# Scaling of x by ScalarE alone in the opening of a gated FFN trunk layer, with the turns of ktiles 8 to 11 moved to the second block's sums

## The chip, the core and the metric

The kernel runs on one core of a Trainium2 chip. The metric is the device time of one execution in microseconds (us); the kernel before has a median of 1994.59 us over three runs.

## What is computed

One decoder layer on x of 256 tokens by 2048 channels in float32: a SwiGLU feed-forward block, a mixer, and a second feed-forward block. Before each, x is normalised and modulated by a vector c. Only the start concerns the change:

```python
mod = (silu(c) @ w_ada + b_ada).reshape(B, 9, 1, D)       # w_ada: 2048 x 18432
h = rms_norm(x, g_ffn1) * (1 + mod[:, 1]) + mod[:, 0]
g, u = split(h @ w_ffn1_gu, 2)                            # w_ffn1_gu: 2048 x 11264
x = x + 0.5 * mod[:, 2] * ((silu(g) * u) @ w_ffn1_down)   # w_ffn1_down: 5632 x 2048
```

No product of h can start before the columns of mod[:, 0] and mod[:, 1] that belong to its channels are summed over all 2048 rows of w_ada.

## The kernel before

**Tiling.** The 2048 channels are 16 ktiles of 128 rows; the 256 tokens are two tiles. Each float32 weight tile `raw` (128 x 1024 per ktile) is split into two reduced-precision halves: `wh`, cast by ScalarE (ACT, L285), and `wl = raw - wh`, by VectorE (DVE, L289). h is split likewise into `hh` and `hl`. TensorE (PE) adds three products per weight tile and token tile, wh·hh, wh·hl and wl·hh, two banks each, all on L304: 12 products of 512 columns for one ktile.

**Order of the products in the opening.** Because the modulation columns arrive in blocks, the first FFN's products run in segments `segs` of (column tile, ktile from, ktile to). The first six segments take ktiles 0 and 1 for six column tiles, the seventh takes ktiles 0 to 5 of column tile 6, and so on. When a segment is done its four PSUM banks are copied out by `evac` (L782), which sets its two groups of four banks free by turns.

**The modulation.** DVE multiplies each row tile of w_ada by its element of silu(c) (`cs`) and adds it up (`ada_acc`, L660/L662). PE then sums `acc` over its 128 rows by products with a column of ones: L764 for the first block (ktiles 0 and 1, all in the opening), L820 in `end` for later blocks. `ada_col` (L668 to L672) adds bias and gain into `mcol`. The second block is ktiles 2 to 5. Its 16 steps are spread over the first 12 turns.

**x.** `x_row` scales two ktiles of x by 1/rms, on ACT (L682) or with `True` as its last argument on DVE (L680). `x_T` turns them on PE by transposes (L688) into a bank, and `x_keep` (L741) copies the turned tile to `xT`, where `h_pair` (L694 to L697) later applies the modulation.

**Order by turns.** All engines follow the written order. `push` queues a ktile's products behind LAG = 2 others; each time one is taken, `turn_` also runs what `at(n, f)` planned for turn n. Turn 12 is where `end` of the second block stands, between the products of ktile 0 and of ktile 1 of the seventh segment.

**Loads.** Weight tiles of 1 MB, of w_ada and of w_ffn1_gu by turns, go through one pool of RAW = 6 buffers, issued in written order by SyncE (SP, L654 and L261); a load waits until the buffer's last reader is done.

Of the kernel before, what the change touches and what calls it, by code (L numbers as in the profile page):

```python
# [16 lines left out]
P = 128  # L17
D = 2048
S = 256
# [24 lines left out]
def trunk_layer(ctx, tc, x, c, w_ada, b_ada, g_ffn1, w_ffn1_gu, w_ffn1_down, g_mix, w_in,  # L44
                pool_mix, pool_scale, w_pool_up, q_gain, k_gain, sinks, rel_bias, w_attn_up,
                w_o, g_ffn2, w_ffn2_gu, w_ffn2_down, pool_w, onehot, out):
    nc = tc.nc
# [7 lines left out]
    def nm(s):  # L55
        uid[0] += 1
        return f"{s}_{uid[0]}"

    def t_(shape, tag, bufs=1, dt=F32):
        return sb.tile(list(shape), dt, tag=tag, bufs=bufs, name=nm(tag))  # L60
# [5 lines left out]
    def bank_at(i, shape):  # L66
        return ps.tile(list(shape), F32, tag=f"bank{i}", name=nm("bank"))

    def bank(shape=(P, CW)):
        for _ in range(4):  # L70
            rr[0] = (rr[0] + 1) % 4
            i = (1 - cur[0]) * 4 + rr[0]
            if i not in held:
                return bank_at(i, shape)
        raise RuntimeError("no bank free in the written order")
# [11 lines left out]
    KG, KB = 3 * KD + PW // P, 6 * KD  # L87
    gcol = const.tile([P, KG], F32, name="gcol")
    bcol = const.tile([P, KB], F32, name="bcol")
# [16 lines left out]
    def push(f):  # L106
        late.append([f])
        pushed[0] += 1
        while len(late) > LAG:
            turn_()  # L110
# [5 lines left out]
    def at(n, f, first=False):  # L116

        fs = plan.setdefault(max(n, done[0]), [])
        fs.insert(0, f) if first else fs.append(f)
# [410 lines left out]
    def turn_T(src, f0, n, actT, at_blocks, at_moves):  # L530


        z = []

        def blocks(t):
            if not z:
                z.append(t_([P, T, n], "raw", RAW))
            nc.vector.transpose(z[0][:, t, :], (src() if callable(src) else src)[:, t, 0:n])  # L538

        def move(i, j):  # L540
            k, m = f0 // P, n // P
            nc.scalar.copy(actT[32 * j:32 * j + 32, k:k + m, :].rearrange("p k (t i r) -> p k t i r", t=T, i=4)[:, :, :, i, :],  # L542
                           z[0][32 * i:32 * i + 32].rearrange("p t (k j r) -> p k t j r", j=4, r=32)[:, :, :, j, :])

        for t in range(T):
            at(at_blocks(t), lambda t=t: blocks(t))
        for q in range(16):
            at(at_moves(q), lambda q=q: move(q // 4, q % 4))
# [108 lines left out]
    def ada_acc(acc, r, kk, first):  # L657
        sc = cs[:, kk:kk + 1]
        if first:
            nc.vector.tensor_scalar_mul(acc, r, sc)  # L660
        else:
            nc.vector.scalar_tensor_tensor(out=acc, in0=r, scalar=sc, in1=acc, op0=ALU.mult, op1=ALU.add)  # L662

    def ada_col(k, n, j, sums):

        m = mcol[:, j, k:k + n]
        if j == 0:
            nc.vector.tensor_tensor(m, sums, bcol[:, k:k + n], ALU.add)  # L668
        else:
            nc.vector.scalar_tensor_tensor(out=m, in0=sums, scalar=1.0, in1=bcol[:, KD + k:KD + k + n],  # L670
                                           op0=ALU.add, op1=ALU.add)
            nc.vector.tensor_tensor(m, m, gcol[:, k:k + n], ALU.mult)  # L672

    def x_row(k, m=2, dve=False):

        xn = t_([P, T, m * P], "t2", T2)
        for t in range(T):
            a, sc = x_sb[:, t, k * P:(k + m) * P], st[:, 4, t:t + 1]
            if dve:
                nc.vector.tensor_scalar_mul(xn[:, t, :], a, sc)  # L680
            else:
                nc.scalar.activation(xn[:, t, :], a, AF.Copy, scale=sc)  # L682
        return xn

    def x_T(xn, b):
        for f in range(xn.shape[2] // P):
            for t in range(T):
                nc.tensor.transpose(b[:, f, t * P:(t + 1) * P], xn[:, t, f * P:(f + 1) * P], ident)  # L688
        return b
# [27 lines left out]
    def first_pe(kk, j):  # L717
        for a in range(2):
            nc.tensor.matmul(bsum[j][a], braw[kk // 4][:, kk % 4, j, a * P:(a + 1) * P], cs[:, kk:kk + 1],
                             start=kk == 0, stop=False)  # L720

    def first_dve(k0):
        for kk in range(k0 + 1, k0 + 4):
            ada_acc(acc0, braw[k0 // 4][:, kk - k0], kk, kk == 1)
# [10 lines left out]
    nc.vector.tensor_reduce(v2, ssq, AX.X, ALU.add)  # L735
    rsqrt2(v2, s0, r0, a0)
    nc.vector.tensor_tensor(st[:, 4, :], r0, a0, ALU.mult)
    xr = [x_row(0), x_row(2), x_row(4, 2, True)]

    def x_keep(b, k):  # L740
        nc.scalar.copy(xT[k], b)  # L741
# [4 lines left out]
    b0 = [x_T(xr[0][:, :, f * P:(f + 1) * P], bank_at(5 + 2 * f, (P, 1, S)))[:, 0, :] for f in range(2)]  # L746
    x_keep(x_T(xr[1], bank_at(6, (P, 2, S))), 2)
    x_keep(x_T(xr[2], bank_at(4, (P, 2, S))), 4)
    xr = [x_row(6, 2, True)]
    for j in (1, 0):  # L750
        first_pe(8, j)
    first_dve(8)
    xr += [x_row(8), x_row(10, 2, True)]
    xT[6] = t_([P, 2, S], "sl", 2)
    x_keep(x_T(xr[0], bank_at(6, (P, 2, S))), 6)
    b = bank_at(4, (P, KG + KB))
    nc.tensor.transpose(b[:, :KG], grow, ident[:KG, :KG])
    nc.tensor.transpose(b[:, KG:], brow, ident[:KB, :KB])
    for j in (1, 0):
        for kk in (13, 14, 15):  # L760
            ada_acc(acc0[:, j], braw[3][:, kk - 12, j], kk, False)
        first_pe(12, j)
        for a in range(2):
            nc.tensor.matmul(bsum[j][a], acc0[:, j, a * P:(a + 1) * P], ones_f[:, 0:1], start=False, stop=True)  # L764
        if j:
            b8 = x_T(xr[1], bank_at(6, (P, 2, S)))
    nc.vector.tensor_copy(gcol, b[:, :KG])
    nc.vector.tensor_copy(bcol, b[:, KG:])
    for j in (1, 0):
        for a in range(2):  # L770
            ada_col(a, 1, j, bsum[j][a])
    b10 = x_T(xr[2], bank_at(4, (P, 2, S)))
    xT[8], xT[10] = t_([P, 2, S], "sh", 2), t_([P, 2, S], "sl", 2)

    segs = [(i, 0, 2) for i in range(6)] + [(6, 0, 6)] + [(i, 2, 6) for i in (5, 4, 3, 2, 1)] + [(0, 2, 10)]
# [2 lines left out]
    def evac(i, k0, k1, s, t, c_):  # L778
        e = slice(c_ * CW, (c_ + 1) * CW)
        a, b = part[i][:, t, e], s.free(t, c_)  # L780
        if k0 == 0:
            nc.scalar.copy(a, b)  # L782
        else:
            nc.vector.tensor_tensor(a, b, a, ALU.add)  # L784
        if k1 == KD:
            if i % 2 or i == NS - 1:
                at(done[0] + 1, lambda a=a: nc.scalar.activation(a, a, AF.Silu))
            else:
                g = part[i + 1][:, t, e]
                nc.vector.tensor_tensor(g, a, g, ALU.mult)  # L790
# [14 lines left out]
    for k, n, need in ((2, 4, 14), (6, 4, 42), (10, 4, 70), (14, 2, 74)):  # L805
# [30 lines left out]
        while q < k + n:  # L836
# [9 lines left out]
                at(n_, lambda q=q, xn=xn, m=m: h_pair(x_T(xn[0], bank((P, m, S))), q, m))  # L846
            q += m

    cur[0] = 1
    n0 = 0  # L850
    for i, k0, k1 in segs:
        s = Set(w_ffn1_gu[0], KD, cols[i], hstat, late=True)
        if n0 == 0:
            raw = t_([P, 2, SW], "raw", RAW)
            for k in range(2):
                nc.sync.dma_start(raw[:, k, :], w_ffn1_gu[0][k * P:(k + 1) * P, cols[i][0]:cols[i][0] + SW])
            h = t_([P, 2, S], "t2", T2)
            wh = [s.hi_half(raw[:, 0, :])]
            mod = lambda a, f: nc.scalar.activation(a[:, f, :], b0[f], AF.Identity, scale=mcol[:, 1, f:f + 1],
                                                    bias=mcol[:, 0, f:f + 1])  # L860
            for f in range(2):
                mod(hh, f)
            wh.append(s.hi_half(raw[:, 1, :]))
            items = [s.prep(f, raw[:, f, :], given=wh[f]) for f in range(2)]
            for f in range(2):
                mod(h, f)
                nc.vector.tensor_tensor(hl[:, f, :], h[:, f, :], hh[:, f, :].bitcast(F32), ALU.subtract)
            x_keep(b8, 8)
            x_keep(b10, 10)

            def first_mm(f, *o, s=s, items=items):
                for t in range(T):
                    s.mm(items[f], t, None, 0, 2, o)

            push(lambda: first_mm(0, 0, 2))
            push(lambda: (first_mm(1, 0), first_mm(0, 1), first_mm(1, 1, 2)))
        else:
            s.pushes(k0, k1, k0, k1)
        n0 = pushed[0] - 1
        for q, (t, c_) in enumerate((t, c_) for t in range(T) for c_ in range(2)):  # L880
            at(n0 + (q // 2 if k1 > 2 else 0), lambda i=i, k0=k0, k1=k1, s=s, t=t, c_=c_: evac(i, k0, k1, s, t, c_), True)
        if k1 == KD and i in (4, 2, 0):
            turn_T(part[i + 1], i // 2 * SW, SW, actT, lambda t: n0 + 2 + t, lambda q: n0 + 5 + q // 2 * (2 if i else 1))
# [187 lines left out]
    for a in range(0, 8, 2):  # L1071
        with_bank(G[0] + 1 + a // 4, (P, 2, S), pool_prod(a),
                  lambda b, a=a: nc.vector.tensor_copy(pT_[0][:, a:a + 2, :], b))
        will(G[0] + 2 + a // 4, 0.7)
    for a in range(8):
        with_bank(G[0] + 4 + a // 2, (P, S), mix_prod(a),
                  lambda b, a=a: nc.scalar.activation(mixT[:, a, :], b, AF.Copy, scale=psc[:, a:a + 1]))
# [258 lines left out]
```

## Time and profile before

| | us |
|---|---|
| median of 3 runs (1993.12 to 1994.67) | 1994.59 |
| profiled execution, its own time | 1996.08 |
| span of that execution, first to last instruction | 1994.3 |
| PE busy | 1972.3 |
| DVE busy | 1513.6 |
| ACT busy | 1091.8 |

The trace gives starts from the span's first instruction. The profiled execution took 1.49 us more than the median run. A busy PE is only a PE with an instruction under way: the clock column PEclk tells whether it ran at its full level (1.00, 2.4 GHz) or at half (0.50, 1.2 GHz).

### The profile page before, as it was taken

The numbers are of one execution on the slowest core, as the hardware profiler recorded it, in microseconds if no ns is written. First come the engines' busy times: TensorE is split into PE (matmuls) and PEld (weight loads), VectorE is DVE, ScalarE is ACT, GpSimd is POOL, SyncE is SP. The second block draws the span as 40 slices with busy tenths as digits, with TensorE's granted clock in tenths as the row PEclk, the third lists the DMA queues.
The fourth block names the chain that finished last, engine by engine and source line by source line (L and its number), as shares of the span: only waits on it lengthen the run. The fifth ranks groups of instructions, "written<-read, shape, count | busy, mean of one in ns | idle before, by whom it ended". The sixth has DMA issues, their size and how long they took to land.

```text
span 1994.3 us, 23770 instructions
## 1 busy us (share of the span) xinstructions
PE 1972.3 (99%) x8873; PEld 1629.3 (82%) x8873; DVE 1513.6 (76%) x1749; ACT 1091.8 (55%) x1484; POOL 26.4 (1%) x51
## 2 busy tenths in 40 slices
PE   7999999999999999999999999999999999999999
PEld 6788888888788888888788888888888888888887
DVE  6898867989999978886889998888455454565655
ACT  6543457664664546446656455645564645565443
POOL 0000000000000000000000000000000000000000
PEclk9999999999999999999999999999999999999999
DMA  9989745899899966876688996598555645466652
GB/s 364 371 314 342 261 164 187 329 337 356 313 363 336 335 230 235 310 281 219 235 292 302 351 311 219 212 356 317 214 189 202 219 170 190 159 225 216 218 185 74
DMA packets 158212, 523.68 MB, mean 263 GB/s; under 512 B 9325, under 2 KB 21509, under 8 KB 157840
## 3 DMA queue, kind: packets, MB, share of 16 engines
q1 hardware_dynamic: 156464, 518.83, 72.7%
q0 software_dynamic: 1632, 3.34, 0.6%
q8 instruction: 69, 1.13, 0.2%
q14 instruction: 47, 0.39, 0.1%
HBM read 520.00 MB, written 2.12 MB: 262 GB/s over the span
## 4 chain that ended last, share of the span: by engine, by line
PE 96%; DVE 2%; DMA 1%; SPq 0%; issue 0%; ACT 0%; DVEq 0%; ACTq 0%
PE bank L304 93%; DVE acc L662 1%; DMA raw<-in_w_ffn_gu_dram 1%; DMA raw<-in_w_ada_dram 0%; DVE wl L289 0%; PE bank L1065 0%; SPq L654 0%; PE bank L820 0%; PE bank L196 0%; PE bank L195 0%; PE bank L357 0%; PE bank L1128 0%; PE bank L1092 0%; PE bank L999 0%; PE bank L1051 0%
## 5 line engine op out<-in xcount | busy, mean ns | idle before, releaser
L285 ACT CAST wh<-raw 128x1024 fp32r<-128x1024 f32 (+2 forms) x711 | 711.1, 1002 | 793.9 <-PE bank L304 739.7
L289 DVE TENSOR_TENSOR wl<-raw,wh 128x1024 fp32r<-128x1024 f32 (+2 forms) x713 | 823.5, 1157 | 418.4 <-ACT wh L285 413.7
L304 PE MATMUL bank<-wh,hl 128*128 128x512 f32 (+1 forms) x2088 | 653.6, 388 | 0.0
L304 PE MATMUL bank<-wh,hh 128*128 128x512 f32 (+1 forms) x2064 | 651.3, 390 | 0.3 <-DVE big L1099 0.3
L304 PE MATMUL bank<-wl,hh 128*128 128x512 f32 (+1 forms) x2064 | 647.5, 389 | 0.6 <-DVE wl L289 0.6
L304 PEld LDWEIGHTS bank<-wh,hl 128*128 128x128 f32 x2088 | 392.7, 188 | 81.3
L304 PEld LDWEIGHTS bank<-wl,hh 128*128 128x128 f32 x2064 | 388.2, 188 | 82.9 <-DVE wl L289 2.9
L304 PEld LDWEIGHTS bank<-wh,hh 128*128 128x128 f32 x2064 | 386.4, 189 | 80.2 <-issue 0.8
L230 DVE SCALAR_TENSOR_TENSOR acc<-raw,cs,acc 128x1024 f32<-128x1024 f32 (+1 forms) x231 | 279.8, 1211 | 0.8
L304 PE MATMUL bank<-wh,sh 128*128 128x512 f32 x656 | 203.7, 390 | 0.0
L304 PE MATMUL bank<-wh,sl 128*128 128x512 f32 x656 | 203.3, 389 | 0.0
L304 PE MATMUL bank<-wl,sh 128*128 128x512 f32 x656 | 203.1, 389 | 0.0
L304 PEld LDWEIGHTS bank<-wh,sl 128*128 128x128 f32 x656 | 123.0, 188 | 26.0 <-DVE sl L394 0.3
L304 PEld LDWEIGHTS bank<-wl,sh 128*128 128x128 f32 x656 | 123.1, 188 | 25.8
L304 PEld LDWEIGHTS bank<-wh,sh 128*128 128x128 f32 x656 | 122.6, 188 | 25.8 <-issue 0.4
L542 ACT COPY big<-raw 32x512 f32<-32x512 f32 (+1 forms) x208 | 121.9, 586 | 4.2
L662 DVE SCALAR_TENSOR_TENSOR acc<-raw,cs,acc 128x1024 f32<-128x1024 f32 (+2 forms) x74 | 77.7, 1052 | 1.0
L394 DVE TENSOR_TENSOR sl<-big,sh 128x512 fp32r<-128x512 f32 x82 | 56.2, 686 | 0.0
L393 ACT CAST sh<-big 128x512 fp32r<-128x512 f32 x82 | 50.7, 618 | 0.0
L784 DVE TENSOR_TENSOR big<-bank,big 128x512 f32<-128x512 f32 x56 | 36.4, 684 | 0.0
L329 ACT ACTIVATE junk<-x_sb 128x512 bf16<-128x512 f32 x24 | 15.2, 632 | 13.9 <-DVE x_sb L421 11.7
L538 DVE STREAM_TRANSPOSE raw<-sg 128x1024 f32<-128x1024 f32 (+1 forms) x20 | 22.7, 1133 | 0.0
(220 smaller groups left out, 802.7 us busy)
## 6 DMA issues: line engine op xcount, KB each, us to landing
raw<-in_w_ffn_gu_dram SPq DMA_DIRECT2D x175, 1024.0 KB, 5.3
raw<-in_w_ada_dram SPq DMA_DIRECT2D x112, 1024.0 KB, 7.2
raw<-in_w_ffn_down_dram SPq DMA_DIRECT2D x86, 1024.0 KB, 6.1
raw<-in_w_in_dram SPq DMA_DIRECT2D x48, 1024.0 KB, 6.8
raw<-in_w_ada_dram SPq DMA_DIRECT2D x64, 512.0 KB, 7.6
raw<-in_w_o_dram SPq DMA_DIRECT2D x15, 1024.0 KB, 7.8
raw<-in_w_pool_up_dram SPq DMA_DIRECT2D x8, 1024.0 KB, 7.9
raw<-in_w_attn_up_dram SPq DMA_DIRECT2D x8, 1024.0 KB, 6.9
```

The lines of the kernel that those rows point to most:

```text
L230: nc.vector.scalar_tensor_tensor(out=a[0], in0=r[0][:, kk % nk, :], scalar=sc, in1=a[0], op0=ALU.mult, op1=ALU.add)
L285: nc.scalar.copy(wh, raw_k)
L289: nc.vector.tensor_tensor(wl[:, e], raw_k[:, e], wh[:, e].bitcast(F32), ALU.subtract)
L304: nc.tensor.matmul(self.banks[t][i], a[:, sl], w[:, o], start=first and q == 0, stop=last and q == 2)
L329: nc.scalar.activation(junk, x_sb[:, t, n * CW:(n + 1) * CW], AF.Square, scale=(D / 2) ** -0.5, accum_out=ssq[:, t, n:n + 1])
L393: nc.scalar.copy(hi, src[:, k:k + n, :])
L394: nc.vector.tensor_tensor(lo, src[:, k:k + n, :], hi.bitcast(F32), ALU.subtract)
L538: nc.vector.transpose(z[0][:, t, :], (src() if callable(src) else src)[:, t, 0:n])
L542: nc.scalar.copy(actT[32 * j:32 * j + 32, k:k + m, :].rearrange("p k (t i r) -> p k t i r", t=T, i=4)[:, :, :, i, :], z[0][32 * i:32 * i + ...
L662: nc.vector.scalar_tensor_tensor(out=acc, in0=r, scalar=sc, in1=acc, op0=ALU.mult, op1=ALU.add)
L784: nc.vector.tensor_tensor(a, b, a, ALU.add)
```

## The change

All of `x_row` goes to ACT; three calls had been on DVE. The copies of the norm weights and biases (`gcol`, `bcol`) go from DVE to ACT. Scaling, turning and keeping ktiles 8 to 11 leave the opening: the rows are scaled at turn 10, turned at turn 12 just ahead of the second block's sums, and kept at turn 13 just ahead of what else stands there. The last products of the first block (`first_pe(12, j)`) now stand together ahead of the sums. The program holds the same calculations before and after.

```diff
@@ -735,7 +735,7 @@
     nc.vector.tensor_reduce(v2, ssq, AX.X, ALU.add)
     rsqrt2(v2, s0, r0, a0)
     nc.vector.tensor_tensor(st[:, 4, :], r0, a0, ALU.mult)
-    xr = [x_row(0), x_row(2), x_row(4, 2, True)]
+    xr = [x_row(0), x_row(2), x_row(4)]
 
     def x_keep(b, k):
         nc.scalar.copy(xT[k], b)
@@ -746,30 +746,27 @@
     b0 = [x_T(xr[0][:, :, f * P:(f + 1) * P], bank_at(5 + 2 * f, (P, 1, S)))[:, 0, :] for f in range(2)]
     x_keep(x_T(xr[1], bank_at(6, (P, 2, S))), 2)
     x_keep(x_T(xr[2], bank_at(4, (P, 2, S))), 4)
-    xr = [x_row(6, 2, True)]
+    xr = [x_row(6)]
     for j in (1, 0):
         first_pe(8, j)
     first_dve(8)
-    xr += [x_row(8), x_row(10, 2, True)]
     xT[6] = t_([P, 2, S], "sl", 2)
     x_keep(x_T(xr[0], bank_at(6, (P, 2, S))), 6)
     b = bank_at(4, (P, KG + KB))
     nc.tensor.transpose(b[:, :KG], grow, ident[:KG, :KG])
     nc.tensor.transpose(b[:, KG:], brow, ident[:KB, :KB])
+    nc.scalar.copy(gcol, b[:, :KG])
+    nc.scalar.copy(bcol, b[:, KG:])
+    for j in (1, 0):
+        first_pe(12, j)
     for j in (1, 0):
         for kk in (13, 14, 15):
             ada_acc(acc0[:, j], braw[3][:, kk - 12, j], kk, False)
-        first_pe(12, j)
         for a in range(2):
             nc.tensor.matmul(bsum[j][a], acc0[:, j, a * P:(a + 1) * P], ones_f[:, 0:1], start=False, stop=True)
-        if j:
-            b8 = x_T(xr[1], bank_at(6, (P, 2, S)))
-    nc.vector.tensor_copy(gcol, b[:, :KG])
-    nc.vector.tensor_copy(bcol, b[:, KG:])
     for j in (1, 0):
         for a in range(2):
             ada_col(a, 1, j, bsum[j][a])
-    b10 = x_T(xr[2], bank_at(4, (P, 2, S)))
     xT[8], xT[10] = t_([P, 2, S], "sh", 2), t_([P, 2, S], "sl", 2)
 
     segs = [(i, 0, 2) for i in range(6)] + [(6, 0, 6)] + [(i, 2, 6) for i in (5, 4, 3, 2, 1)] + [(0, 2, 10)]
@@ -845,6 +842,21 @@
                     n_ += 1
                 at(n_, lambda q=q, xn=xn, m=m: h_pair(x_T(xn[0], bank((P, m, S))), q, m))
             q += m
+
+
+    def two_rows():
+        xr[:] = [x_row(8), x_row(10)]
+
+    def two_turns():
+        xr[:] = [x_T(a, bank((P, 2, S))) for a in xr]
+
+    def two_keeps():
+        for a, k in zip(xr, (8, 10)):
+            x_keep(a, k)
+
+    at(10, two_rows)
+    at(12, two_turns, True)
+    at(13, two_keeps, True)
 
     cur[0] = 1
     n0 = 0
@@ -865,8 +877,6 @@
             for f in range(2):
                 mod(h, f)
                 nc.vector.tensor_tensor(hl[:, f, :], h[:, f, :], hh[:, f, :].bitcast(F32), ALU.subtract)
-            x_keep(b8, 8)
-            x_keep(b10, 10)
 
             def first_mm(f, *o, s=s, items=items):
                 for t in range(T):
```

On DVE in the opening these rows stood or now stand between the scaling by 1/rms and the first modulation column (acc_126 is the first block's sum, raw_110 to raw_116 its tiles of w_ada):

```order
-L680 TENSOR_SCALAR t_29_164<-x_sb,st 128x256 x2
 L662 SCALAR_TENSOR_TENSOR acc_126<-raw_110,cs,acc_126 128x512 x3
-L680 TENSOR_SCALAR t_34_192<-x_sb,st 128x256 x2
 L662 SCALAR_TENSOR_TENSOR acc_126<-raw_113,cs,acc_126 128x512 x3
-L680 TENSOR_SCALAR t_36_205<-x_sb,st 128x256 x2
 L662 SCALAR_TENSOR_TENSOR acc_126<-raw_116,cs,acc_126 128x256 x6
-L767 COPY gcol<-bank_215 128x56
-L768 COPY bcol<-bank_215 128x96
 L670 SCALAR_TENSOR_TENSOR mcol<-bank_124,bcol 128x1
 L672 TENSOR_TENSOR mcol<-mcol,gcol 128x1
```

Eight instructions leave DVE between those sums.

On ACT at turns 10 to 12 of the kernel before (raw_518 holds ktiles 0 and 1 of the seventh segment, banks 524 to 527 the sixth segment's result):

```order
L285 CAST wh_520<-raw_518 128x1024
L285 CAST wh_544<-raw_518 128x1024
L782 COPY gate_103<-bank_527 128x512
L782 COPY gate_103<-bank_526 128x512
L782 COPY gate_103<-bank_525 128x512
L782 COPY gate_103<-bank_524 128x512
L285 CAST wh_567<-raw_565 128x1024
```

and in the changed kernel, where raw_500 and banks 506 to 509 are the same things:

```order
L285 CAST wh_502<-raw_500 128x1024
L682 ACTIVATE t_107_526<-x_sb,st 128x256 x2
L682 ACTIVATE t_108_529<-x_sb,st 128x256 x2
L285 CAST wh_532<-raw_500 128x1024
L779 COPY gate_103<-bank_509 128x512
L779 COPY gate_103<-bank_508 128x512
L779 COPY gate_103<-bank_507 128x512
L779 COPY gate_103<-bank_506 128x512
L285 CAST wh_555<-raw_553 128x1024
```

Four scalings now stand between the two casts, ahead of the copies out of the banks.

On PE at turn 12, before (bank_587 takes the second block's sums; the trace lists each of these float32 products as two):

```order
L304 MATMUL bank_573<-wl_521,hh_105 128x512
L304 MATMUL bank_574<-wl_521,hh_105 128x512
L820 MATMUL bank_587<-ones_f,acc_290 128x1 x8
L304 MATMUL bank_571<-wh_544,hh_105 128x512
L304 MATMUL bank_572<-wh_544,hh_105 128x512
```

and after:

```order
L304 MATMUL bank_561<-wl_503,hh_105 128x512
L304 MATMUL bank_562<-wl_503,hh_105 128x512
L688 MATMUL bank_575<-ident,t_107_526 128x128 x4
L688 MATMUL bank_580<-ident,t_108_529 128x128 x4
L817 MATMUL bank_585<-ones_f,acc_272 128x1 x8
L304 MATMUL bank_559<-wh_532,hh_105 128x512
L304 MATMUL bank_560<-wh_532,hh_105 128x512
```

Eight transposes now stand between ktile 0's last product and the sums. Their banks come from the group that the sixth segment used: by the order of the pool, bank_575 follows bank_507, bank_580 follows bank_508, and bank_585 follows bank_509.

## Rows read from the trace of the kernel before

**Rows 1.** The page: the chain of work that ended last, as shares of the span by engine.

```profile
PE 96%; DVE 2%; DMA 1%; SPq 0%; issue 0%; ACT 0%; DVEq 0%; ACTq 0%
```

**Rows 2.** The chain that ended last in the opening, in order of time: start, us, what.

```profile
43.38 10.49 DMA raw<-in_w_ffn_gu_dram
...
65.92 2.41 PE bank L820 x16
68.33 59.97 PE bank L304 x252
```

**Rows 3.** Busy time by stretch: PE, PEld, DVE, ACT, POOL (instructions), PEclk, DMA share, GB/s.

```profile
30.00:36.00 6.00, 6.00 (x28) 4.98 (x27) 5.03 (x7) 4.31 (x8) 0.00 (x0) 1.00 1.05 397
...
48.00:54.00 6.00, 6.00 (x29) 4.95 (x27) 5.82 (x6) 3.17 (x7) 0.00 (x0) 1.00 1.04 396
...
66.00:72.00 6.00, 6.00 (x25) 5.23 (x26) 2.44 (x6) 3.13 (x6) 3.15 (x8) 0.60 1.04 395
...
76.00:80.00 4.00, 4.00 (x19) 3.33 (x18) 2.47 (x3) 2.11 (x2) 0.00 (x0) 1.00 0.84 284
```

**Rows 4.** SP's issues in order of time (start, us from the first issue's start to the last one's end), then the loads issued at 52.4 and at 53.07 us with us from issue to landing.

```profile
51.94 0.88 SPq L654 DMA_DIRECT2D raw<-in_w_ada_dram  x2
53.07 4.79 SPq L261 DMA_DIRECT2D raw<-in_w_ffn_gu_dram  x2
...
raw<-in_w_ada_dram SPq DMA_DIRECT2D x1, 512.0 KB, 9.5
...
raw<-in_w_ffn_gu_dram SPq DMA_DIRECT2D x1, 1024.0 KB, 11.3
```

**Rows 5.** ACT in order of time around the second block's sums: start, us, instructions, and in brackets the idle time before with what ended it.

```profile
53.96 2.00 ACT L285 CAST wh<-raw 128x1024 fp32r<-128x1024 f32 x2 [1.33 <-DMA raw<-in_w_ffn_gu_dram]
...
59.23 2.01 ACT L285 CAST wh<-raw 128x1024 fp32r<-128x1024 f32 x2 [1.16 <-DMA raw<-in_w_ffn_gu_dram]
61.45 2.06 ACT L782 COPY gate<-bank 128x512 f32<-128x512 f32 x4 [0.21 <-PE bank L304]
64.49 1.04 ACT L285 CAST wh<-raw 128x1024 fp32r<-128x1024 f32 x1 [0.98 <-DMA raw<-in_w_ffn_gu_dram]
68.83 1.09 ACT L694 ACTIVATE t<-big,mcol 128x256 f32<-128x256 f32 x2 [3.30 <-DVE mcol L668]
```

**Rows 6.** DVE in order of time in the same stretch.

```profile
55.04 1.23 DVE L289 TENSOR_TENSOR wl<-raw,wh 128x1024 fp32r<-128x1024 f32 x1 [0.80 <-ACT wh L285]
...
61.03 1.22 DVE L289 TENSOR_TENSOR wl<-raw,wh 128x1024 fp32r<-128x1024 f32 x1
62.17 1.28 DVE L662 SCALAR_TENSOR_TENSOR acc<-raw,cs,acc 128x1024 f32<-128x1024 f32 x1
63.36 1.22 DVE L289 TENSOR_TENSOR wl<-raw,wh 128x1024 fp32r<-128x1024 f32 x1
64.50 1.28 DVE L662 SCALAR_TENSOR_TENSOR acc<-raw,cs,acc 128x1024 f32<-128x1024 f32 x1
65.69 1.22 DVE L289 TENSOR_TENSOR wl<-raw,wh 128x1024 fp32r<-128x1024 f32 x1
```

**Rows 7.** PE in order of time in the same stretch; a row's us reach to its last product's end, which overlaps the next row.

```profile
61.25 0.62 PE L304 MATMUL bank<-wh,hh 128*128 128x512 f32 x2
61.70 0.61 PE L304 MATMUL bank<-wh,hl 128*128 128x512 f32 x2
...
63.80 0.62 PE L304 MATMUL bank<-wl,hh 128*128 128x512 f32 x2
65.92 2.41 PE L820 MATMUL bank<-ones_f,acc 128*128 128x1 f32 x16 [1.50 <-DVE acc L662]
68.19 1.20 PE L304 MATMUL bank<-wh,hh 128*128 128x512 f32 x2
...
73.46 0.88 PE L304 MATMUL bank<-wh,hh 128*128 128x512 f32 x2
74.18 0.62 PE L304 MATMUL bank<-wh,hl 128*128 128x512 f32 x2
```

**Rows 8.** The opening, all engines, in order of time.

```profile
15.74 1.71 ACT L682 ACTIVATE t<-x_sb,st 128x256 f32<-128x256 f32 x4 [1.02 <-DVE st L737]
15.80 0.62 DVE L680 TENSOR_SCALAR t<-x_sb,st 128x256 f32<-128x256 f32 x2
16.31 3.01 PE L688 MATMUL bank<-ident,t 128*128 128x128 f32 x12
...
20.06 0.64 PE L688 MATMUL bank<-ident,t 128*128 128x128 f32 x4
...
24.73 0.21 DVE L767 COPY gcol<-bank 128x56 f32<-128x56 f32 x1
24.86 0.25 DVE L768 COPY bcol<-bank 128x96 f32<-128x96 f32 x1
...
27.51 1.20 PE L304 MATMUL bank<-wh,hh 128*128 128x512 f32 x2
...
29.47 0.59 ACT L741 COPY sh<-bank 128x512 f32<-128x512 f32 x1
```

**Rows 9.** PE around the third block's sums, in order of time.

```profile
128.14 1.84 PE L820 MATMUL bank<-ones_f,acc 128*128 128x1 f32 x16
129.84 0.72 PE L304 MATMUL bank<-wh,hh 128*128 128x512 f32 x2
```

## The prediction

> **What bounds the kernel now.** I read the chain that ended last first: 96% of it is PE [rows 1], and from 68.33 us on it is PE without a break for 60 us [rows 2]. A change in the opening can therefore save only what lets PE begin its unbroken run earlier, or run it at full clock earlier. So the question is what holds PE up to about 74 us.
>
> Followed back from 68.33, the chain goes through the second block's sums (65.92) to a load that took 10.49 us to land, issued at 43.38 [rows 2]. One MB at about 397 GB/s needs 1.05 / 0.397 = 2.6 us, so that load had some 4 MB of others ahead of it or beside it. The busy time by stretch says the same: the DMA engines are full (1.04 to 1.05) from 30 to 72 us and show their first slack only at 76 to 80 us (0.84, 284 GB/s) [rows 3]. The loads of this stretch run at their full rate however early they are asked for.
>
> ACT's rows show where this binds: at 53.96, 59.23 and 64.49 its casts start when a tile lands, after 1.33, 1.16 and 0.98 us of idling [rows 5]. The first of these makes DVE wait 0.80 us, until 55.04 [rows 6]. From there DVE's rows follow each other closely up to the second block's last addition at 64.50 [rows 6], and PE, done with ktile 0 at about 64.4, idles 1.50 us for it [rows 7]. The clock then falls: the stretch 66 to 72 us has a mean clock of 0.60 [rows 3]. The product pairs from 68.19 to 73.46 come 0.85 to 1.0 us apart, against 0.45 us between 61.25 and 61.70 [rows 7].
>
> **The opening itself.** The change takes six scalings (0.62 us for each two) and the copies of 0.21 and 0.25 us off DVE, ahead of the first modulation column: 3 x 0.62 + 0.46 = 2.3 us [rows 8]. It also takes eight transposes off PE and two copies of 0.59 us off ACT [rows 8], but these lie partly in the shadow of DVE's chain. I estimate that the first dense product, now at 27.51 [rows 8], comes about 2.3 us earlier. The scalings cost ACT 1.71 / 4 = 0.43 us each [rows 8], where it waits anyway (1.02 us before 15.74 alone).
>
> How much of this 2.3 us lasts? The load issued at 53.07 landed 11.3 us later, at 64.4, and ACT's cast followed it at 64.49 [rows 4, 5]. The last tile of the second block, issued at about 52.4, landed 9.5 us later, at 61.9, and DVE's addition from it began at 62.17 [rows 4, 6]. Even with everything before it done, DVE could not have begun that addition more than 0.27 us sooner; the next cast could gain 0.1 us. The order of the loads on SP is the same before and after. Between nothing and 2.3 us (if the DMA engines had slack after all) I take **0.0 us** kept: the earlier start turns into longer waits of ACT and DVE for tiles up to 53.96.
>
> **The wait for the second block.** Three things move here.
>
> First, ACT scales four rows between its casts: 4 x 0.43 = 1.7 to 1.8 us. The cast that began at 59.23 ends at about 60.25, the scalings at 62.1, the second cast at 63.1. Queued behind that cast is DVE's subtraction, which began at 63.36 [rows 6]: covered, by about 0.25 us. The four bank copies, 2.06 us from 61.45 on [rows 5], move to 63.1. The first transposes need the third of the banks that these copies clear (bank_507), free at 63.1 + 3 x 0.52 = 64.65. PE is ready at about 64.4, so it waits 0.25 us. The next cast follows the copies, at 65.15 instead of 64.49, and DVE's subtraction from it ends at about 67.4 instead of 66.9. The modulation behind that needs the sums, not ready before 67.7, so this is covered by 0.3 us.
>
> Second, eight transposes at 0.64 / 4 = 0.16 us [rows 8] run on PE from 64.65 to 65.93, in the idle time. The sums began at 65.92 [rows 7]; I charge **+0.1 us**, between 0.0 (the bank comes in time) and +0.6 (PE waits for all four copies, until 65.15).
>
> Third, the clock. In the rows of before, PE did nothing for 1.50 us and then 2.27 us of one-column products, until 68.19 [rows 7]; in this stretch the clock fell. Around the third block the same products alone, 128.14 to 129.84, left it at full level: they took 1.70 us, and the pairs behind them are again close [rows 9]. With transposes in most of the idle time, the new stretch is nearer to the second than to the first. Do transposes keep the clock up? At 16.31 twelve of them took 3.01 us, 0.25 us each, and right behind that run, at 20.06, four took 0.64 us [rows 8]. So the clock rose on little else than transposes, although the profile prints no half level for the first 20 us. I take it that they count, and that the clock holds. Then the sums take 1.70 instead of 2.27 us (**-0.57**). The seven pairs from 68.19 to 74.18 take 7 x 0.453 = 3.17 instead of 5.99 us (**-2.82**). By this the second block's h is needed at about 70.5 for ktile 2. ACT's modulation began 0.64 us after the dense products did (68.83 against 68.19) [rows 5, 7]; it would now begin at about 68.3 and with its cast needs 1.75 us, to 70.1: just in time.
>
> The Trainium skill, "TensorE: Matmul & The Clock Gate", section "Part 4: PE-mode transpose", says that a transpose does not count as PE activity for the clock. By that rule the clock would fall here as before and the sum would be +0.1 us; the row at 16.31 speaks against it.
>
> Last, the two kept copies (2 x 0.6 us on ACT) now stand before the modulation of ktiles 4 and 5. PE needs that two ktiles later, at least 5.4 us, so it is covered.
>
> **Sum.** 0.0 + 0.1 - 0.57 - 2.82 = **-3.3 us**, against the profiled execution's 1996.08 us: 1992.8. That execution lies 1.49 us above the median run, so against the median of 1994.59 the time is **1991.3 us**, 0.17% less. About 0.2% (4.0 us) is what a measurement here can tell from no change, so this counts as within it. The bounds of its terms put it between 1990.2 and 1992.4.
>
> **Rivals.**
>
> *The clock falls all the same.* The stretch without dense products still lasts from 64.4 to about 68, and the three runs of before differ by 1.5 us, which fits a clock that does not fall alike in each. Then the terms of the clock go and +0.1 us stays, between -1 and +1 with the point at which it falls: **1994.7 us**.
>
> *The opening's gain lasts.* If the DMA rate gives way when more loads wait, part of the 2.3 us comes on top of the clock: -3.3 - 2.3, **1989.0 us**. Against it speaks that the DMA share is 1.04 in every stretch while the rate stays at 395 to 398 GB/s [rows 3].
>
> *Slower, by the banks.* If ACT's first cast at the wait comes later than 59.5, the copies clear the bank later than 64.9, the transposes overrun DVE's last addition, and all that PE does then is on the path. If the clock has by then fallen, eight transposes at 0.25 us are 2.0 us and the sums, twice 1.70, 3.4 us. From 64.9 on this ends at 70.3 instead of 68.19; with dense products at half speed for as long as before it is +2.1 us, **1996.7 us**. The point that decides is whether the bank is free before DVE's last addition ends at 65.8.
>
> *The change does nothing at the wait*, because the rows of x come too late for PE's idle time. They are ready at 62.1, so I give this no chance of its own.
>
> **How the numbers follow.** The clock holds, opening gone: 0.53. The clock falls: 0.30. Opening kept too: 0.10. Slower by banks: 0.07. The range reaches from 1989.6, which takes in a part of the third case, to 1995.2, which takes in the second: about 0.85. Faster by over 0.2% means below 1990.6: most of the third case and a fifth of the first, 0.20. Slower by over 0.2% means above 1998.6, half of the last: 0.04. The rest, 0.76, is within.
>
> **What would show it.** Right: ACT's waits for tiles of w_ffn1_gu begin before 53.96 and are longer; the last addition of the second block still ends at 65.5 to 66.0; the transposes lie just ahead of the sums; PEclk reads 1.00 from 66 to 74. Wrong: an addition that ends at 63 to 64 (the loads came earlier), a fall of the clock in that stretch, or PE waiting for a bank behind ACT's copies for more than 0.5 us.

## The result and the profile after

The changed kernel is slower: a median of 1999.26 us over 8 runs (1997.53 to 2000.8), against 1993.3 us for the kernel before over 8 runs. The ratio is 1.0025, with a 95% interval from 1.0016 to 1.0034. That is +6.0 us by the medians, where -3.3 us was forecast, and outside the range of 1989.6 to 1995.2. The kernel before scatters by itself: in the later comparisons its median is 1994.5 to 1994.8 us, so the loss may be nearer 4.5 us than 6.

The opening itself went much as forecast. These are rows of the changed kernel around the wait for the second block's sums, PE first, then ACT and DVE (start, us, instructions, in brackets the idle time before and what ended it). They answer to [rows 5 to 7].

```profile
63.89 0.61 PE L304 MATMUL bank<-wl,hh 128*128 128x512 f32 x2
64.44 1.10 PE L688 MATMUL bank<-ident,t 128*128 128x128 f32 x8
65.93 1.95 PE L817 MATMUL bank<-ones_f,acc 128*128 128x1 f32 x16 [0.39 <-DVE acc L662]
67.74 1.01 PE L304 MATMUL bank<-wh,hh 128*128 128x512 f32 x2
68.54 1.05 PE L304 MATMUL bank<-wh,hl 128*128 128x512 f32 x2
...
72.60 0.62 PE L304 MATMUL bank<-wh,hl 128*128 128x512 f32 x2
```

```profile
54.06 2.00 ACT L285 CAST wh<-raw 128x1024 fp32r<-128x1024 f32 x2 [1.80 <-DMA raw<-in_w_ffn_gu_dram]
...
59.35 1.05 ACT L285 CAST wh<-raw 128x1024 fp32r<-128x1024 f32 x1 [1.35 <-DMA raw<-in_w_ffn_gu_dram]
60.30 1.71 ACT L682 ACTIVATE t<-x_sb,st 128x256 f32<-128x256 f32 x4
61.91 1.04 ACT L285 CAST wh<-raw 128x1024 fp32r<-128x1024 f32 x1
62.85 2.02 ACT L779 COPY gate<-bank 128x512 f32<-128x512 f32 x4
```

```profile
55.14 1.23 DVE L289 TENSOR_TENSOR wl<-raw,wh 128x1024 fp32r<-128x1024 f32 x1 [1.27 <-ACT wh L285]
...
64.60 1.28 DVE L662 SCALAR_TENSOR_TENSOR acc<-raw,cs,acc 128x1024 f32<-128x1024 f32 x1
```

The sums begin at 65.93 us, before at 65.92: the 1.57 us by which the first dense product comes sooner are gone, and ACT and DVE stand longer for the tile that lands at 54 us (1.80 and 1.27 us, before 1.33 and 0.80). The eighth pair of products behind the sums, which began at 74.18 us before [rows 7], begins at 72.60: the changed kernel is then 1.6 us ahead of the one profiled execution of before (whether the change did that is taken up below). So what cost it time lies behind the part that I had worked out. The next rows are PE's in the changed kernel near 128 us, to be read against [rows 9], and near 200 us.

```profile
126.55 1.84 PE L817 MATMUL bank<-ones_f,acc 128*128 128x1 f32 x16
129.00 0.85 PE L304 MATMUL bank<-wh,hh 128*128 128x512 f32 x2 [0.62 <-DVE mcol L668]
129.64 1.06 PE L304 MATMUL bank<-wh,hl 128*128 128x512 f32 x2
130.50 1.06 PE L304 MATMUL bank<-wl,hh 128*128 128x512 f32 x2
...
198.46 0.47 PE L304 MATMUL bank<-wh,hh 128*128 128x512 f32 x1 [0.27 <-DVE mcol L668]
...
204.44 0.63 PE L688 MATMUL bank<-ident,t 128*128 128x128 f32 x4 [0.51 <-DVE big L781]
```

PE waits 0.62 us after the third block's sums, until DVE has written the modulation columns, and the product pairs that follow come up to 0.86 us apart instead of 0.46: the clock has fallen, to 0.50 from 130 to 132 us. Before, these products followed the sums without a wait, at full clock. Two smaller waits follow near 200 us, and one of 1.15 us near 971, where the kernel before waits 0.30. Busy time by stretch shows the clock (columns as in [rows 3], PEclk is the third from the end):

```profile
128.00:134.00 6.00, 5.38 (x19) 4.33 (x19) 3.47 (x8) 5.05 (x8) 0.00 (x0) 0.72 0.88 332
```

**What the products wait for.** Banks of PSUM are picked by a counter, `rr`, in the function `bank`, one further at each pick, in the group that the running segment does not use. The changed kernel calls it two more times, once for each of the moved turns. In the opening these turns had named their banks (`bank_at`) and left the counter alone. So every later pick is two banks further. By the written order of the program:

| pick | bank before | bank after | when the next segment's products or copies want it |
|---|---|---|---|
| third block's sums | 6 | 4 | bank 4 first, bank 6 third of four |
| fourth block's sums | 3 | 1 | bank 1 second, bank 3 last |
| turning of ktiles 12 and 13 (turn 59) | 4 | 6 | bank 4 is copied out at one turn, bank 6 at the next |

The sums lie in their bank until DVE has read them into `mcol`. In bank 4 they stand in the way of the next segment's very first product.

### The profile page after: what moved, and what is told of

The parts are those of the page before. It is cut to its first block, busy times and chain, and to the rows that moved or that the text cites. A ratio compares the mean times of both kernels' runs of the same rounds, so it can differ in the third digit from the quotient of the medians.

```text
span 1998.1 us, 23764 instructions
## 1 busy us (share of the span) xinstructions
PE 1975.8 (99%) x8873; PEld 1630.2 (82%) x8873; DVE 1511.9 (76%) x1741; ACT 1092.9 (55%) x1492; POOL 26.3 (1%) x51
## 4 chain that ended last, share of the span: by engine, by line
PE 94%; DVE 2%; DMA 2%; ACT 1%; issue 1%; SPq 0%; ACTq 0%; DVEq 0%
PE bank L304 91%; DMA raw<-in_w_ffn_down_dram 1%; DVE wl L289 1%; DMA raw<-in_w_ffn_gu_dram 1%; DMA raw<-in_w_ada_dram 1%; DVE acc L662 0%; PE bank L1075 0%; PE bank L196 0%; PE bank L195 0%; PE bank L817 0%; PE bank L357 0%; ACT wh L285 0%; PE bank L1138 0%; PE bank L1102 0%; PE bank L688 0%
```

## The experiments

Theory A is this shift of the counter. Theory B is the moved work itself: its loads, and ACT's copies that come later.

**The changed kernel with the later picks as before.**

```diff
             b = bank((P, 2, n))
+            if k == 2:
+                rr[0] = (rr[0] + 2) % 4
```

> The changed kernel, but the counter that picks banks skips two after the second block's sums, so that every later pick is the bank it was before. Theory A (the loss comes from the two extra picks, which shift every later pick by two banks): the waits of PE at 128.4 and 203 us and the fall of the clock behind the first of them are gone, and the time is 1.5 to 3 us below before, 1990.3 to 1991.8. Theory B (the loss comes from the moved work itself, by loads or by ScalarE's later copies): the time stays at 1998 to 2000.

Measured: 1994.92 us median of 11 runs, ratio to before 0.9998 [0.9989, 1.0007]. The slowdown is gone. PE's rows of this kernel behind the third block's sums have no wait and no slow pairs:

```profile
126.99 1.84 PE L819 MATMUL bank<-ones_f,acc 128*128 128x1 f32 x16
128.69 0.72 PE L304 MATMUL bank<-wh,hh 128*128 128x512 f32 x2
129.25 0.63 PE L304 MATMUL bank<-wh,hl 128*128 128x512 f32 x2
```

Theory B falls. But theory A's numbers are not met either: 1.5 to 3 us below before was expected, and the kernel stands level with it.

**The kernel before with the shift alone.** The same two lines in the kernel before.

> The kernel before, with nothing changed but the counter that picks banks: it skips two after the second block's sums. Theory A: 4 to 7 us slower than before (1997 to 2000), with PE waiting for a modulation column behind the third block's sums and for a bank near 203 us. Theory B: no change, within 1 us of before.

Measured: 1999.59 us, ratio 1.0021 [1.0012, 1.0030], before on the same chip 1994.77: +4.8 us with no work moved. PE waits the same 0.62 us at the third sums, and here the clock falls behind the fourth as well (PE in order of time; then busy time in the stretches around both):

```profile
130.41 0.70 PE L304 MATMUL bank<-wh,hh 128*128 128x512 f32 x2 [0.62 <-DVE mcol L668]
...
199.88 0.59 PE L304 MATMUL bank<-wh,hh 128*128 128x512 f32 x1 [0.27 <-DVE mcol L668]
200.27 1.06 PE L304 MATMUL bank<-wh,hl 128*128 128x512 f32 x2
```

```profile
128.00:134.00 6.00, 5.38 (x28) 4.60 (x27) 3.11 (x7) 3.66 (x6) 0.00 (x0) 0.82 1.02 395
...
198.00:204.00 6.00, 5.73 (x24) 4.61 (x24) 1.80 (x5) 3.67 (x7) 1.47 (x2) 0.72 0.67 233
```

**The shift in three parts**, each in the kernel before: the third block's sums alone, the fourth's alone, and all picks behind the fourth's.

```diff
+            if k == 6:
+                rr[0] = (rr[0] + 2) % 4
             b = bank((P, 2, n))
+            if k == 6:
+                rr[0] = (rr[0] + 2) % 4
```

The second has `k == 10` in both places. In the last of the three only the second addition stands, with `k == 10`.

> The kernel before, with only the third block's sums in the bank that they have in the changed kernel (the first bank that the next segment's products need, instead of its third). All other picks as before. Theory A1 (a wait of 0.6 us for the modulation column, and a clock that then falls in many executions): 1.5 to 2.5 us slower than before. Theory A2 (the wait alone matters): 0.6 us slower. If the loss lies elsewhere: within 0.3 us of before.

Measured: 1997.3 us against 1994.72, +2.6 us, ratio 1.0015 [1.0006, 1.0024]. PE's rows:

```profile
127.61 1.19 PE L304 MATMUL bank<-wh,hh 128*128 128x512 f32 x2 [0.61 <-DVE mcol L668]
128.60 1.05 PE L304 MATMUL bank<-wh,hl 128*128 128x512 f32 x2
129.45 1.05 PE L304 MATMUL bank<-wl,hh 128*128 128x512 f32 x2
130.31 0.90 PE L304 MATMUL bank<-wh,hh 128*128 128x512 f32 x2
131.05 0.63 PE L304 MATMUL bank<-wh,hl 128*128 128x512 f32 x2
```

In the kernel before, where the sums began at 128.14 us and the first pair at 129.84 [rows 9], the fifth pair is

```profile
131.79 0.63 PE L304 MATMUL bank<-wh,hl 128*128 128x512 f32 x2
```

With the wait of 0.61 us the first pair comes 2.45 us after the sums' start (125.16 us) instead of 1.70, and the four gaps between pairs take 3.44 us instead of 1.95: 0.75 and 1.5 us, together 2.2. So A1 holds, though the median is 0.1 us beyond its bounds, and the larger part of the price is the clock. The clock falls here in the three profiles with this wait and in none of the eight without it.

> The kernel before, with only the fourth block's sums in the bank that they have in the changed kernel (the second that the next segment needs, instead of its last). Theory A1: a wait of about 0.3 us and a fall of the clock in some executions, 0.5 to 1.5 us slower. Theory A2: 0.3 us slower.

Measured: 1995.18 us, +0.5 us, ratio 1.0002 [0.9994, 1.0011]: not to be told from no change. The profile shows the wait (0.28 us) and no fall of the clock.

> The kernel before, with the banks of the sums as before and every pick behind the fourth block's sums shifted by two. What the first two runs leave of the loss must show here: 1 to 2 us slower than before, with PE waiting 0.5 us or more for DVE's copies out of banks near 203 us and 970 us. If it is within 0.3 us, the sums are all of it.

Measured: 1996.85 us, +2.1 us, ratio 1.0011 [1.0002, 1.0020]. Two of its waits make up nearly all of it: 1.00 us before the turn near 202 us, where the kernel before has none, and 1.15 us near 968, where that waits 0.30 (last row).

```profile
202.37 0.63 PE L688 MATMUL bank<-ident,t 128*128 128x128 f32 x4 [1.00 <-DVE big L784]
...
967.81 0.70 PE L304 MATMUL bank<-wh,hh 128*128 128x512 f32 x2 [1.15 <-DVE big L1101]
```

```profile
967.32 0.50 PE L304 MATMUL bank<-wh,hh 128*128 128x512 f32 x1 [0.30 <-DVE big L1099]
```

The parts add up to 2.6 + 0.5 + 2.1 = 5.2 us, the whole shift to 4.8.

**ScalarE's part alone.** The kernel before with all scaling and both copies on ACT, the turns left in the opening (in the edit the calls of `x_row` lose their `True`, and the two copies become `nc.scalar.copy` where they stand).

> The kernel before, with all scaling of x and the copies of gains and biases on ScalarE, but the turns of ktiles 8 to 11 left in the opening. Theory A, with the opening bound by loads up to 54 us: within 0.5 us of before, PE's first dense product 0.5 to 1.5 us earlier, the second block's last addition ending at 65.6 to 66.0 as before. If the opening's gain lasts instead: 1 us or more below before.

Measured: 1994.84 against 1994.77 us, ratio 1.0001 [0.9993, 1.0010]. PE's first dense product begins 1.51 us sooner, and the wait for the second block is as before, to be read against [rows 7]:

```profile
26.00 1.20 PE L304 MATMUL bank<-wh,hh 128*128 128x512 f32 x2
...
66.18 2.38 PE L820 MATMUL bank<-ones_f,acc 128*128 128x1 f32 x16 [1.51 <-DVE acc L662]
```

ACT waits 2.28 us for the tile that lands at 54 us, where the kernel before waits 1.33 [rows 5]. So the opening's gain is lost to the loads, as the prediction said.

**The move alone**, with DVE's scalings of ktiles 4 to 7 and its two copies kept and the later picks as before.

> The changed kernel with VectorE doing its scalings of ktiles 4 to 7 and the copies of gains and biases again, and with the later picks of banks as before. So only the move of ktiles 8 to 11 into the wait is left. Theory A: the same as the run with the same banks, within 0.7 us, since what is saved in the opening is lost to loads. If ScalarE's part matters: 1 us or more above it.

Measured: 1994.52 us, ratio 0.9995 [0.9986, 1.0004]; 0.4 us from the run with the same banks, as expected.

**More transposes in the wait.** What is left is why the kernel with the same banks gains nothing at the wait it fills. Its clock still falls there. The edit turns the second tile twice:

```diff
-        xr[:] = [x_T(a, bank((P, 2, S))) for a in xr]
+        rows = list(xr)
+        xr[:] = [x_T(a, bank((P, 2, S))) for a in rows]
+        x_T(rows[1], xr[1])
```

> The changed kernel with the later banks as before, and the four transposes of ktiles 10 and 11 done twice (the second time with the same result), so that 12 transposes instead of 8 stand in the wait for the second block's sums. Theory C (transposes count as work for the clock, and what is left of its fall is the rest of the idle time): PE's idle time there goes from 0.4 us to none, the clock falls in fewer executions, and the median is 0.5 to 1.5 us below the run with the same banks. If transposes do not count: the same or 0.2 us slower.

Measured: 1993.28 us against 1994.72, ratio 0.9994 [0.9985, 1.0003]. PE in order of time in the kernel with the same banks (8 transposes), then in this one (12), then the busy time of this one in the stretch behind:

```profile
64.84 1.10 PE L688 MATMUL bank<-ident,t 128*128 128x128 f32 x8
66.35 1.95 PE L819 MATMUL bank<-ones_f,acc 128*128 128x1 f32 x16 [0.41 <-DVE acc L662]
...
69.16 1.00 PE L304 MATMUL bank<-wl,hh 128*128 128x512 f32 x2
69.96 1.05 PE L304 MATMUL bank<-wh,hh 128*128 128x512 f32 x2
```

```profile
64.67 1.53 PE L688 MATMUL bank<-ident,t 128*128 128x128 f32 x12
66.18 1.95 PE L819 MATMUL bank<-ones_f,acc 128*128 128x1 f32 x16
67.99 0.71 PE L304 MATMUL bank<-wh,hh 128*128 128x512 f32 x2
68.53 0.62 PE L304 MATMUL bank<-wh,hl 128*128 128x512 f32 x2
```

```profile
66.00:72.00 6.00, 6.00 (x36) 5.05 (x35) 3.03 (x7) 3.39 (x7) 3.35 (x8) 1.00 1.04 394
```

With 12 the idle time is gone and the clock stays at 1.00.

**Only filling.** The kernel before with nothing moved; 12 transposes whose result nobody reads are added at the wait.

```diff
+    def fill():
+        f = bank_at((1 - cur[0]) * 4 + 3, (P, 2, S))
+        for _ in range(3):
+            x_T(x_sb[:, :, 0:2 * P], f)
+
+    at(12, fill, True)
```

> The kernel before with nothing moved: 12 transposes of unused x, into a bank that nobody reads, are added at the wait for the second block's sums, and no later pick of a bank changes. Theory C (what the wait costs is the fall of the clock behind it, and transposes keep the clock up): 1 to 2 us faster than before, near 1993.3, with PEclk at 1.00 from 66 to 74 us. If the gain of the run with more turns came from taking work out of the opening: the same as before or up to 0.3 us slower.

Measured: 1993.26 us against 1994.53, ratio 0.9996 [0.9987, 1.0005]. The clock holds (PE in order of time, then the busy time in the stretch):

```profile
64.65 1.47 PE L688 MATMUL bank<-ident,x_sb 128*128 128x128 f32 x12
66.05 1.92 PE L820 MATMUL bank<-ones_f,acc 128*128 128x1 f32 x16
67.83 0.72 PE L304 MATMUL bank<-wh,hh 128*128 128x512 f32 x2
```

```profile
66.00:72.00 6.00, 6.00 (x36) 5.20 (x35) 2.92 (x6) 3.50 (x6) 3.47 (x9) 1.00 1.04 397
```

This gives the same 1.3 to 1.4 us as 12 transposes of moved work. By the intervals neither median can be told from the kernel before with certainty, but the single executions differ more plainly. Under 1993.7 us lie 18 of the 81 executions of the kernel before that the experiments were compared with, 3 of 11 for each of the two kernels with eight transposes (the same banks, the move alone), and 8 of 11 for each of the two with twelve. So the gain comes with the clock that holds, not with the work that left the opening.

## Why the prediction was wrong

**The step that failed** is the list of what the change adds. It asked what the two new `bank` calls wait for, worked out which banks they and the sums get at turn 12, and stopped there. It did not follow the counter on to the next picks. This missing term measured +4.8 us alone. In the changed kernel it is 4.3 us by the medians (1999.26 against 1994.92 us for the run with the same banks, which stands level with before). All of the slowdown lies in it. The rival "slower, by the banks" named the banks at the wait itself, where nothing went wrong: the transposes began at 64.44 us with no wait to be seen.

**The opening: right.** 0.0 us kept, and the run with ScalarE's part alone shows it (1.51 us sooner at the first product, the same median). The first product's lead of 2.3 us was too high; the changed kernel has 1.57 us.

**The sums' start, +0.1 us: right** (65.93 against 65.92).

**The clock, -0.57 and -2.82 us: a second term that failed, by its size.** Twelve transposes, with or without a use, were followed by a clock that holds. Eight with 0.4 us of idling behind them were not, in any of the three kernels profiled with them: PEclk is 0.72, 0.77 and 0.72 from 66 to 72 us. By the medians these eight gained nothing (1994.92 and 1994.52 us against 1994.77 for before), where 3.4 us was forecast. The prediction had given a clock that falls all the same a chance of 0.30, and for this stretch that rival came true.

The forecast was sized on one execution, and this stretch does not run alike in each. Up to the third block's sums, the runs with the third or the fourth sums shifted have the instructions of the kernel before. These are their second block's sums and the eighth pair behind them, first with the fourth sums shifted, then with the third:

```profile
66.05 1.92 PE L824 MATMUL bank<-ones_f,acc 128*128 128x1 f32 x16 [1.50 <-DVE acc L662]
...
72.72 0.62 PE L304 MATMUL bank<-wh,hl 128*128 128x512 f32 x2
```

```profile
66.13 1.92 PE L824 MATMUL bank<-ones_f,acc 128*128 128x1 f32 x16 [0.94 <-DVE acc L662]
...
71.21 0.62 PE L304 MATMUL bank<-wh,hl 128*128 128x512 f32 x2
```

From the sums' start to this pair it is 6.67 and 5.08 us here, 8.26 in the profile that the sum started from (65.92 to 74.18), and 6.67 in the changed kernel (65.93 to 72.60). PEclk from 66 to 72 us is 0.72, 1.00, 0.60 and 0.72. So the changed kernel's lead of 1.6 us is one that the kernel before has over itself in another execution, and that eight transposes shorten the fall is not shown. The times agree: of the 81 executions of before, 21 have a mean granted clock of 1.000 (median 1993.3 us), 34 have 0.999 (1994.7) and 13 have 0.996 (1996.3). The profiled execution has 0.996 and took 1996.08 us. A gain read from it alone is more than the median can give: 12 transposes gained 2.9 us against that execution, and 1.4 us by the medians. The prediction had seen that it lay 1.5 us above the median run, and took all of the forecast gain off the median even so.

"I take it that they count" leaned on twelve transposes at 16.31 us and four in 0.64 us right behind [rows 8]. That does not repeat. In eight of the eleven profiles four transposes behind the same twelve take 1.09 us, as here in the kernel that was only filled, whose opening is that of before:

```profile
16.18 3.01 PE L688 MATMUL bank<-ident,t 128*128 128x128 f32 x12
...
20.55 1.09 PE L688 MATMUL bank<-ident,t 128*128 128x128 f32 x4
```

That transposes raise the clock is therefore not shown; that twelve of them hold it rests on the two last experiments.

What stays open: in the changed kernel's profiled execution PE loses another 1.1 us near 553 to 562 us, to halves of h that come late behind a load of w_ffn1_down. The run with only the third sums shifted, whose banks there are as before, shows a loss of 2.1 us in the same place, and the one with all later picks shifted shows none. So it is not the banks there; what makes that load late in some executions was not tried. What decides for how long the clock falls behind the second block's sums in an execution stays open too.

## What to carry to other kernels

When a change adds or removes a call that advances a shared counter (banks, buffers taken in turn), list the later picks too: the instruction that is hurt may stand a hundred microseconds behind the edit. Sums that wait for another engine to read them belong in the bank that the next products need last. And before a gain is counted from work moved into a wait, ask whether the engines that got free have anything to do earlier: here loads at their full rate took all of it, and only filling the whole wait lowered the times. A price read from one profiled execution holds for executions of its kind: look at how the times of all of them lie before it is taken off the median.

## What the runs showed of the hardware

- A wait of 0.6 us on PE behind 1.7 us of one-column products brought the clock from full to half in three profiles; the same products without the wait left it full in the other eight (0.72 or 0.82 against 1.00 around 128 to 134 us). The clock's part of the price, 1.5 us in the run with the third sums shifted, is twice the 0.75 us that the wait itself cost.
- The length of a wait did not decide alone. In that run an idle time of 0.94 us ahead of the second block's sums left the clock full, and 0.61 us behind the third block's brought it down. A wait of 0.27 or 0.28 us behind the fourth block's sums was followed by a fall in one of three profiles (0.72 from 198 to 204 us).
- 12 float32 transposes that nobody used held the clock at 1.00 from 66 to 72 us, where the profile of the kernel before has 0.60 and those of two runs with its opening have 0.72 and 1.00. The Trainium skill, "TensorE: Matmul & The Clock Gate", "Part 4: PE-mode transpose", says that the full clock does not engage for transposes, which do not count as busy in the same way. For holding a clock that is already full the executions here speak against it (16 of 22 under 1993.7 us with twelve transposes, 18 of 81 in the kernel before); for raising it no run here does clearly.
